# Two plain-form indices at the head of each feed-forward layer, and one index made ahead of each round of down products

## The chip, the cores and the metric

The kernel runs on one core of a Trainium2 chip. The metric is the device time of one execution in microseconds (us), lower is better; times are medians over runs of the kernel.

## What is computed

Two transformer-like blocks follow one another, each of two layers. The change touches the feed-forward part of the first block's two layers only:

```python
for l in range(DEPTH):                       # DEPTH = 2
    ...                                      # mixer: attention and a recurrent branch
    hn = rms_norm(h, norm_ffn_g[l])
    g, u = jnp.split(hn @ w_gu[l], [D_FF], axis=-1)      # D_FF = 2816, D_MODEL = 1024
    h = h + (jax.nn.silu(g) * u) @ w_down[l]
return h[:, N_META:, :]                      # then the second block
```

Everything is float32. Activations are held transposed: 1024 features as 8 tiles of 128 partitions, and 528 tokens (16 + 512) as columns. In the second layer only the last 512 tokens are needed, so that layer works on 512 columns.

## The kernel before

**Precision.** A float32 product is made of three matmuls: each operand is divided into a rounded part and a remainder (`hi`, `lo`), and `mm3` (L104) adds hi x hi, hi x lo, lo x hi. `split` (L188) makes the two: ScalarE copies `hi` (L189), VectorE subtracts (L190). Weights go the same way: `weight` (L95) loads 128 x 1024 values, copies on ScalarE (L99), subtracts on VectorE (L101). The tiles `wraw`, `whi`, `wlo` have 3 buffers each.

**One index.** The 2816 hidden features are 22 indices of 128. An index needs two weight tiles, gate and up. The plain way would be, for each of the two tiles and each half of the tokens (`n0`, `n1`, 264 or 256 columns), 8 feature tiles x 3 matmuls: 2 x 2 x 24 = 96 matmuls. The kernel uses seven products of quarters in place of eight (`seven`, L160): 7 x 4 x 3 = 84 matmuls. For that it needs sums of weight quarters, made on GpSimd in `halves4` (L133, four operations, L144 to L147), and sums of operand quarters, made once per layer (`ts`, divided into `th`, `tl`). The seven products land in PSUM (`av` one bank; `two`, 3 buffers of two banks), are added up on VectorE into `quarters` (L178 to L185), go through Silu on ScalarE (L691) and a product on GpSimd (L692), and are divided by `split` into `yh{i}`, `yl{i}`.

**The head of the layer.** After the norm (L229 to L244, with a chain of small VectorE operations, `rsqrt`, L203 to L216) VectorE scales each of 8 feature tiles into `g` (L655), first for `n0`, then for `n1`; `split` writes `xa` (`xh_all`, `xl_all`). The seven-product form needs, over `n1`, differences in place of some values: `g[k]` over `n1` is replaced for k < 4 (L668), and three sums for each k < 4 are made by GpSimd (L664, L672) and VectorE (L665).

**The down products.** The 22 indices run in chunks of 6, 6, 5, 5. After the last index of a chunk, for each of 8 output tiles m, a weight tile `w1dn` is loaded, both halves are multiplied with the chunk's `yh`, `yl` on TensorE, and VectorE adds the result to `h` (L704).

**Order.** The framework places waits and orders the instructions of each engine at compile time by a priority that follows the program text, with operations taken ahead of their place where its planner sees them ready. In the trace GpSimd's weight sums of the first two indices (L144 to L147) run beside the norm. Each engine then executes its own instructions in that fixed order, and every DMA of weights is issued by one queue (SP).

Of the kernel before, what the change touches and what calls it, by code (L numbers as in the profile page):

```python
# [9 lines left out]
F32 = mybir.dt.float32  # L10
F32R = mybir.dt.float32r
BF = mybir.dt.bfloat16
I32 = mybir.dt.int32
AF = mybir.ActivationFunctionType
# [6 lines left out]
T = S + NM  # L21
# [25 lines left out]
def both_blocks(ctx: ExitStack, tc: tile.TileContext, xT, cst, par1, w1in, w1out, w1gu, w1dn, wgate,  # L47
                memT, pos, par2, rel, w2in, w2mix, w2mq, w2mkv, w2mo, w2f1, w2f2, out):
    nc = tc.nc
# [4 lines left out]
    psum = None  # L54

    def open_psum(name):
        nonlocal psum, banks
        banks.close()
        banks = ExitStack()
        psum = banks.enter_context(tc.tile_pool(name=name, bufs=1, space=bass.MemoryType.PSUM))  # L60
# [2 lines left out]
    EARLY = 4  # L63
    BANKS = {"mm": 3, "sc": 2, "tr": 1, "av": 1, "bc": 1}
    EXTRA = {"mix1": None, "ff1": None, "mix2": "tr", "cross": "tr", "ff2": None}
    extra, turns = None, {}

    ALL = [(0, 264), (264, 528)]
    REAL = [(16, 528)]
# [22 lines left out]
    def f(ap):  # L92
        return ap.bitcast(F32)

    def weight(src, kt=8, eng=None):  # L95
        raw = wpool.tile([128, 8, 128], F32, name="wraw", bufs=3)
        nc.sync.dma_start(raw[:, :kt], src)
        hi = wpool.tile([128, 8, 128], F32R, name="whi", bufs=3)
        nc.scalar.copy(hi[:, :kt], raw[:, :kt])  # L99
        lo = wpool.tile([128, 8, 128], F32R, name="wlo", bufs=3)  # L100
        (eng or nc.vector).tensor_sub(lo[:, :kt], raw[:, :kt], f(hi[:, :kt]))  # L101
        return hi, lo

    def mm3(ps, wh, wl, xh, xl, first, last):  # L104
        nc.tensor.matmul(ps, wh, xh, start=first, stop=False)  # L105
        nc.tensor.matmul(ps, wh, xl, start=False, stop=False)  # L106
        nc.tensor.matmul(ps, wl, xh, start=False, stop=last)  # L107

    def bank(name):
        n = turns[name] = turns.get(name, 0) + 1  # L110
        if name == extra and n % (BANKS[name] + 1) == 0:
            name = "bc"
        return psum.tile([128, 512], F32, name=name, bufs=BANKS[name])
# [74 lines left out]
    def split(hi, lo, x):  # L188
        nc.scalar.copy(hi, x)  # L189
        nc.vector.tensor_sub(lo, x, f(hi))  # L190
# [68 lines left out]
    def tables():  # L259

        with tc.tile_pool(name="tab", bufs=1, side="right") as tb:
            halfpi = tb.tile([128, 1], F32)
            nc.vector.memset(halfpi, math.pi / 2)
            pi = tb.tile([128, S], I32)
            nc.sync.dma_start(pi, bass.AP(tensor=pos.tensor, offset=pos.offset, ap=[[0, 128], [1, S]]))
            pf = tb.tile([128, S], F32)
            nc.vector.tensor_copy(pf, pi)
            for n in range(2):
                ang = tb.tile([128, S], F32, name="ang")
                tn = tb.tile([128, S], F32, name="tn")  # L270
                if n:
                    co = sm.tile([128, S], F32, name="co")
                    si = sm.tile([128, S], F32, name="si")
                else:
                    co, si = cos1[:, :S], sin1[:, :S]
                nc.vector.tensor_scalar(ang, pf, inv[:, 2 * n:2 * n + 1], None, op0=OP.mult)
                nc.vector.tensor_scalar(tn, ang, 1 / (2 * math.pi), 12582912.0, op0=OP.mult, op1=OP.add)
                nc.vector.tensor_scalar(tn, tn, -12582912.0, None, op0=OP.add)
                for part in TWO_PI:
                    nc.vector.scalar_tensor_tensor(ang, tn, -part, ang, op0=OP.mult, op1=OP.add)  # L280
                nc.vector.tensor_scalar(ang, ang, math.pi - 1e-7, -(math.pi - 1e-7), op0=OP.min, op1=OP.max)
                nc.scalar.activation(si, ang, AF.Sin)
                nc.vector.tensor_scalar(si, si, inv[:, 2 * n + 1:2 * n + 2], None, op0=OP.mult)
                nc.scalar.activation(ang, ang, AF.Abs)
                nc.scalar.activation(co, ang, AF.Sin, bias=halfpi, scale=-1.0)
                tabs.append((co, si))
# [24 lines left out]
    for l in range(2):  # L311
# [4 lines left out]
        with ExitStack() as lay:  # L316
# [322 lines left out]
            with ExitStack() as ffn:  # L639
                share("ff1")  # L640
                open_psum("psum_f")
                ff = ffn.enter_context(tc.tile_pool(name="ff", bufs=1))
                r2 = small.tile([128, T], F32, name="rbc", bufs=1)
                for p, a, b in rnorm(small, sumsq(small, h, l0, T), l0, T, one2, D, 1e-6):
                    nc.scalar.copy(r2[:, a:b], p)
                half = (T - l0) // 2
                n0, n1 = slice(l0, l0 + half), slice(l0 + half, T)
                th, tl = (ff.tile([128, 4, 3, half], F32R, name=n) for n in ("th", "tl"))
                with tc.tile_pool(name="tq", bufs=1, side="right") as tq:
                    g = [None] * 8  # L650

                    def scaled(k, n):
                        if g[k] is None:
                            g[k] = tq.tile([128, T], F32, name=f"g{k}")
                        nc.vector.scalar_tensor_tensor(g[k][:, n], h[k][:, n], col(G_FFN + k), r2[:, n], op0=OP.mult, op1=OP.mult)  # L655

                    for k in range(8):
                        scaled(k, n0)
                        split(xa[k][0][:, n0], xa[k][1][:, n0], g[k][:, n0])
                    ts = [tq.tile([128, 3, half], F32, name=f"tt{k}") for k in range(4)]  # L660
                    for k in range(4):
                        scaled(k + 4, n1)
                        scaled(k, n1)
                        nc.gpsimd.tensor_sub(ts[k][:, 0], g[k][:, n1], g[k][:, n0])  # L664
                        nc.vector.tensor_sub(ts[k][:, 1], g[k + 4][:, n1], ts[k][:, 0])  # L665
                        split(th[:, k, :2], tl[:, k, :2], ts[k][:, :2])
                    for k in range(4):
                        nc.gpsimd.tensor_sub(g[k][:, n1], g[k + 4][:, n1], g[k][:, n1])  # L668
                        split(xa[k][0][:, n1], xa[k][1][:, n1], g[k][:, n1])
                    for k in range(4):  # L670
                        split(xa[k + 4][0][:, n1], xa[k + 4][1][:, n1], g[k + 4][:, n1])
                        nc.gpsimd.tensor_sub(ts[k][:, 2], g[k + 4][:, n0], ts[k][:, 1])  # L672
                        split(th[:, k, 2], tl[:, k, 2], ts[k][:, 2])
                quarters = [[[x[k][:, n] for k in ks] for x in zip(*xa)]
                            for ks, n in ((range(4), n0), (range(4, 8), n0), (range(4, 8), n1), (range(4), n1))]
                turned = [[[t[:, k, j] for k in range(4)] for t in (th, tl)] for j in range(3)]
                rhs = quarters[0], quarters[1], turned[1], turned[0], quarters[3], quarters[2], turned[2]
                if l == 1:
                    sm = blk2.enter_context(tc.tile_pool(name="sm", bufs=1, side="right"))
                fy = ffn.enter_context(tc.tile_pool(name="fy", bufs=1, side="right"))  # L680
                f0 = 0
                for nf in (6, 6, 5, 5):
                    if l == 1 and f0 == 6:
                        tables()
                    ys = []
                    for i in range(nf):
                        w = halves4(ff, w1gu[l, 2 * (f0 + i)], w1gu[l, 2 * (f0 + i) + 1])
                        e = seven(ff, w, rhs, half, 2 if l else 3)
                        sg, su = (e[:, o:o + 2].rearrange("p a b -> p (a b)") for o in (0, 2))
                        sl = ff.tile([128, T], F32, name="sl", bufs=1)  # L690
                        nc.scalar.activation(sl[:, l0:], sg, AF.Silu)  # L691
                        nc.gpsimd.tensor_mul(su, su, sl[:, l0:])  # L692
                        hi = fy.tile([128, T], F32R, name=f"yh{i}")
                        lo = fy.tile([128, T], F32R, name=f"yl{i}")
                        split(hi[:, l0:], lo[:, l0:], su)
                        ys.append((hi, lo))
                    for m in range(8):
                        w = weight(w1dn[l, m, :, f0:f0 + nf], nf)
                        ps = pair_of_banks()[:, :, :half]
                        for j, n in enumerate((n0, n1)):  # L700
                            for k, (yh, yl) in enumerate(ys):
                                mm3(ps[:, j], w[0][:, k], w[1][:, k], yh[:, n], yl[:, n], k == 0, k == nf - 1)
                        t = h[m][:, l0:].rearrange("p (a b) -> p a b", a=2)
                        nc.vector.tensor_add(t, t, ps)  # L704
                    f0 += nf
# [617 lines left out]
```

## Time and profile before

| | us |
|---|---|
| median of 3 runs | 2926.09 |
| lowest, highest | 2921.92, 2927.14 |
| the profiled execution's own time | 2924.17 |
| its span, first to last instruction | 2922.4 |
| mean granted TensorE clock (1 is 2.4 GHz) | 0.978 |
| feed-forward part of layer 0, from the norm's first matmul | about 279 to 680 |
| feed-forward part of layer 1 | about 927 to 1330 |

The profile is of one execution. An engine's "busy" is time in which it executes. A matmul's own duration overlaps that of its neighbours, so counts of matmuls per stretch are the better measure of TensorE's progress. PE is TensorE, DVE VectorE, ACT ScalarE, POOL GpSimd. "PEclk" is the clock that was granted, as a share of 2.4 GHz; 0.5 is 1.2 GHz.

### The profile page before, as it was taken

What the parts mean: (1) busy time and instruction counts of PE and PEld (TensorE: products, weight loads), DVE (VectorE), ACT (ScalarE), POOL (GpSimd) and SP (SyncE); (2) the same over time, 40 slices, a digit from 0 to 9 for tenths busy, and PEclk for the clock granted to TensorE, in tenths of its full rate; (3) what the DMA queues carried; (4) which work ended last, traced back from release to release, by engine and by line L of the source; (5) the groups of instructions that cost most, each with busy time, mean ns of one, the idle gap of its engine ahead of it and who ended that gap; (6) DMA issues with size and microseconds to landing.
All of it is one profiled execution on the core that took longest, in us unless ns stands there. A gap on an engine that the chain in (4) does not pass through costs nothing.

```text
span 2922.4 us, 46047 instructions
## 1 busy us (share of the span) xinstructions
PE 2763.0 (95%) x17604; PEld 2465.2 (84%) x17604; DVE 1939.8 (66%) x3702; ACT 1319.7 (45%) x2354; POOL 752.5 (26%) x647
## 2 busy tenths in 40 slices
PE   8988799999997899999999999999989999999998
PEld 7887799999875899998788888888877898888887
DVE  7887856667888855666988564333589875643335
ACT  6664433346664433343675434322346754433323
POOL 0012635450112644542202021111322120311112
PEclk9998899999998899999999999999999999999999
DMA  4332132223332233324613322333245242233222
GB/s 146 84 82 73 55 101 91 90 85 101 103 85 72 73 100 93 91 82 126 170 59 124 107 67 92 94 94 98 89 120 152 66 131 87 65 95 100 94 94 65
DMA packets 98813, 277.39 MB, mean 95 GB/s; under 512 B 13601, under 2 KB 20257, under 8 KB 98593
## 3 DMA queue, kind: packets, MB, share of 16 engines
q1 hardware_dynamic: 98592, 274.45, 31.2%
q8 instruction: 139, 2.28, 0.3%
q14 instruction: 82, 0.66, 0.1%
HBM read 241.82 MB, written 2.10 MB: 83 GB/s over the span
## 4 chain that ended last, share of the span: by engine, by line
PE 73%; DVE 13%; issue 5%; POOL 4%; ACT 3%; DMA 1%; SPq 0%; ACTq 0%; DVEq 0%; POOLq 0%
PE mm L106 16%; PE mm L107 16%; PE mm L105 16%; PE two L107 4%; PE two L105 4%; PE two L106 4%; POOL quarters L692 2%; PE av L105 1%; PE av L106 1%; PE av L107 1%; PE av L229 1%; POOL ws L147 1%; DVE wlo L101 1%; DVE wlo L190 1%; PE bc L927 1%
## 5 line engine op out<-in xcount | busy, mean ns | idle before, releaser
L99 ACT CAST whi<-wraw 128x1024 fp32r<-128x1024 f32 (+3 forms) x388 | 375.0, 970 | 635.9 <-PE mm L106 496.4
L105 PE MATMUL mm<-xh_all,whi 128*128 128x512 f32 (+2 forms) x1696 | 588.3, 349 | 14.6 <-ACT xh_all L328 7.1
L106 PE MATMUL mm<-xl_all,whi 128*128 128x512 f32 (+2 forms) x1696 | 591.2, 350 | 1.3 <-DVE xl_all L845 0.8
L107 PE MATMUL mm<-xh_all,wlo 128*128 128x512 f32 (+2 forms) x1696 | 588.4, 348 | 0.0
L101 DVE TENSOR_TENSOR wlo<-wraw,whi 128x1024 fp32r<-128x1024 f32 (+3 forms) x365 | 442.0, 1211 | 205.5 <-ACT whi L99 203.1
L105 PEld LDWEIGHTS mm<-xh_all,whi 128*128 128x128 f32 x1696 | 321.2, 190 | 53.1 <-ACT xh_all L328 7.1
L106 PEld LDWEIGHTS mm<-xl_all,whi 128*128 128x128 f32 x1696 | 322.1, 190 | 38.4 <-DVE xl_all L845 1.6
L107 PEld LDWEIGHTS mm<-xh_all,wlo 128*128 128x128 f32 x1696 | 323.0, 191 | 34.6
L1206 POOL TENSOR_TENSOR r<-r 128x512 f32<-128x512 f32 (+1 forms) x70 | 101.8, 1455 | 532.3 <-ACT r L1205 532.3
L105 PE MATMUL two<-yh,whi 128*128 128x264 f32 (+1 forms) x704 | 203.1, 290 | 17.8 <-ACT yh L189 16.3
L107 PE MATMUL two<-yh,wlo 128*128 128x264 f32 (+1 forms) x704 | 201.8, 288 | 0.0
L106 PE MATMUL two<-yl,whi 128*128 128x264 f32 (+1 forms) x704 | 201.3, 287 | 0.0
L106 PE MATMUL two<-tl,whi 128*128 128x264 f32 (+1 forms) x528 | 152.6, 289 | 4.3 <-DVE tl L190 4.3
L105 PE MATMUL two<-th,whi 128*128 128x264 f32 (+1 forms) x528 | 151.5, 288 | 5.0 <-ACT th L189 4.9
L107 PE MATMUL two<-th,wlo 128*128 128x264 f32 (+1 forms) x528 | 152.1, 288 | 4.1 <-DVE wlo L190 4.1
L105 PEld LDWEIGHTS two<-yh,whi 128*128 128x128 f32 x704 | 136.0, 194 | 20.4 <-ACT yh L189 18.0
L190 DVE TENSOR_TENSOR wlo<-wraw,whi 128x1024 fp32r<-128x1024 f32 x88 | 135.4, 1538 | 18.8 <-ACT whi L189 18.8
L773 DVE TENSOR_TENSOR hall<-hall,mm 128x512 f32<-128x512 f32 (+1 forms) x82 | 46.6, 568 | 146.0 <-PE mm L107 146.0
L106 PEld LDWEIGHTS two<-yl,whi 128*128 128x128 f32 x704 | 135.8, 193 | 0.1
L107 PEld LDWEIGHTS two<-yh,wlo 128*128 128x128 f32 x704 | 135.8, 193 | 0.0
L144 POOL TENSOR_TENSOR ws<-wraw 128x512 f32<-128x512 f32 x44 | 64.9, 1476 | 201.9 <-DMA wraw<-w1gu 129.0
L189 ACT CAST whi<-wraw 128x1024 fp32r<-128x1024 f32 x88 | 92.3, 1049 | 54.1 <-PE two L106 51.2
(718 smaller groups left out, 7574.5 us busy)
## 6 DMA issues: line engine op xcount, KB each, us to landing
wraw<-w2f SPq DMA_DIRECT2D x128, 512.0 KB, 3.9
wraw<-w1gu SPq DMA_DIRECT2D x88, 512.0 KB, 3.5
wraw<-w2in SPq DMA_DIRECT2D x44, 512.0 KB, 3.7
wraw<-w1in SPq DMA_DIRECT2D x40, 512.0 KB, 3.5
wraw<-w2mkv SPq DMA_DIRECT2D x32, 512.0 KB, 3.5
wraw<-w1dn SPq DMA_DIRECT2D x32, 384.0 KB, 3.1
wraw<-w1dn SPq DMA_DIRECT2D x32, 320.0 KB, 2.9
wraw<-w1out SPq DMA_DIRECT2D x32, 256.0 KB, 2.8
```

What stands on the lines that cost most here:

```text
L99: nc.scalar.copy(hi[:, :kt], raw[:, :kt])
L101: (eng or nc.vector).tensor_sub(lo[:, :kt], raw[:, :kt], f(hi[:, :kt]))
L105: nc.tensor.matmul(ps, wh, xh, start=first, stop=False)
L106: nc.tensor.matmul(ps, wh, xl, start=False, stop=False)
L107: nc.tensor.matmul(ps, wl, xh, start=False, stop=last)
L144: nc.gpsimd.tensor_add(s[:, 4:], r2[:, :4], r2[:, 4:])
L147: nc.gpsimd.tensor_sub(s4, r1[:, 4:], s[:, :4])
L189: nc.scalar.copy(hi, x)
L190: nc.vector.tensor_sub(lo, x, f(hi))
L692: nc.gpsimd.tensor_mul(su, su, sl[:, l0:])
L773: nc.vector.tensor_add(X(m, a, b), X(m, a, b), p)
L1206: nc.gpsimd.tensor_mul(r[:, a:b], r[:, a:b], r[:, a:b])
```

## The change

- The operands of both halves are scaled and divided first, in plain form, on VectorE and ScalarE. All sums of operand quarters (16 operations, four for each k < 4) then go to GpSimd; before, four of the 16 were VectorE's.
- `early()` makes the layer's indices 0 and 1 in plain form, 8 groups of 24 matmuls from four weight tiles; its PSUM tiles are halves of `two`. Silu is read from PSUM, and the product with Silu is VectorE's.
- The divisions of the sums (`th`, `tl`) and the rewritten `xa` over `n1` for k < 4 stand behind `early()`.
- The three engines' work on index 2's weights is kept behind the last division of the plain operands (`issue_after`; on GpSimd behind a copy of one column, `spot`).
- Chunks are 5, 5, 4, 4, 4, and before a chunk's down products the next chunk's first index is made.

```diff
     def open_psum(name):
-        nonlocal psum, banks
+        nonlocal psum, banks, paired, halves
+        paired, halves = name == "psum_f", None
...
+    halves = None
+
     def bank(name):
+        nonlocal halves
+        if name == "mm" and paired:
+            if halves is None:
+                got = psum.tile([128, 2, 512], F32, name="two", bufs=3)
+                halves = got[:, 1]
+                return got[:, 0]
+            got, halves = halves, None
+            return got
...
+                spot = ff.tile([128, 1], F32, name="spot")
+                firsts = [ff.tile([128, 4, half], F32, name="quarters", bufs=2 if l else 3) for _ in range(2)]
+
+                def early():
+
+                    ws = [weight(w1gu[l, t]) for t in range(3)]
+                    for t, n, j in ((0, n0, 0), (1, n0, 0), (2, n0, 0), (0, n1, 1), (1, n1, 1), (2, n1, 1), (3, n0, 0), (3, n1, 1)):
+                        if t == 3 and j == 0:
+                            ws.append(weight(w1gu[l, 3]))
+                        e = firsts[t // 2]
+                        for p, a, b in proj(ws[t], xa, [(n.start, n.stop)]):
+                            if t % 2:
+                                nc.vector.tensor_mul(e[:, 2 + j], e[:, j], p)
+                            else:
+                                nc.scalar.activation(e[:, j], p, AF.Silu)
+
...
-                    for k in range(8):
-                        scaled(k, n0)
-                        split(xa[k][0][:, n0], xa[k][1][:, n0], g[k][:, n0])
+                    for n in (n0, n1):
+                        for k in range(8):
+                            scaled(k, n)
+                            hi, lo = xa[k]
+                            after = [nc.scalar.copy(hi[:, n], g[k][:, n]),
+                                     nc.vector.tensor_sub(lo[:, n], g[k][:, n], f(hi[:, n]))]
+                    after.append(nc.gpsimd.tensor_copy(spot, g[7][:, T - 1:T]))
                     ts = [tq.tile([128, 3, half], F32, name=f"tt{k}") for k in range(4)]
                     for k in range(4):
-                        scaled(k + 4, n1)
-                        scaled(k, n1)
                         nc.gpsimd.tensor_sub(ts[k][:, 0], g[k][:, n1], g[k][:, n0])
-                        nc.vector.tensor_sub(ts[k][:, 1], g[k + 4][:, n1], ts[k][:, 0])
-                        split(th[:, k, :2], tl[:, k, :2], ts[k][:, :2])
+                        nc.gpsimd.tensor_sub(ts[k][:, 1], g[k + 4][:, n1], ts[k][:, 0])
+                        nc.gpsimd.tensor_sub(g[k][:, n1], g[k + 4][:, n1], g[k][:, n1])
+                        nc.gpsimd.tensor_sub(ts[k][:, 2], g[k + 4][:, n0], ts[k][:, 1])
+                    early()
                     for k in range(4):
-                        nc.gpsimd.tensor_sub(g[k][:, n1], g[k + 4][:, n1], g[k][:, n1])
+                        split(th[:, k], tl[:, k], ts[k])
                         split(xa[k][0][:, n1], xa[k][1][:, n1], g[k][:, n1])
-                    for k in range(4):
-                        split(xa[k + 4][0][:, n1], xa[k + 4][1][:, n1], g[k + 4][:, n1])
-                        nc.gpsimd.tensor_sub(ts[k][:, 2], g[k + 4][:, n0], ts[k][:, 1])
-                        split(th[:, k, 2], tl[:, k, 2], ts[k][:, 2])
...
-                f0 = 0
-                for nf in (6, 6, 5, 5):
-                    if l == 1 and f0 == 6:
-                        tables()
-                    ys = []
-                    for i in range(nf):
-                        w = halves4(ff, w1gu[l, 2 * (f0 + i)], w1gu[l, 2 * (f0 + i) + 1])
+                made = []
+
+                def index(i):
+                    if i < 2:
+                        su = firsts[i][:, 2:4].rearrange("p a b -> p (a b)")
+                    else:
+                        with ExitStack() as order:
+                            if i == 2:
+                                for ins in after:
+                                    order.enter_context(tc.issue_after(ins.ins))
+                            w = halves4(ff, w1gu[l, 2 * i], w1gu[l, 2 * i + 1])
...
+                    hi = fy.tile([128, T], F32R, name=f"yh{i % 6}")
+                    lo = fy.tile([128, T], F32R, name=f"yl{i % 6}")
+                    split(hi[:, l0:], lo[:, l0:], su)
+                    made.append((hi, lo))
+
+                f0 = 0
+                for nf in (5, 5, 4, 4, 4):
+                    if l == 1 and f0 == 5:
+                        tables()
+                    while len(made) < min(f0 + nf + 1, 22):
+                        index(len(made))
+                    ys = made[f0:f0 + nf]
```

## Rows read from the trace of the kernel before

**Rows 1.** The page: the span, and each engine's busy time, share and instructions
```profile
span 2922.4 us, 46047 instructions
PE 2763.0 (95%) x17604; PEld 2465.2 (84%) x17604; DVE 1939.8 (66%) x3702; ACT 1319.7 (45%) x2354; POOL 752.5 (26%) x647
```
**Rows 2.** TensorE's waits, layer 0, 288 to 680: total us, times, longest
```profile
PE two L105 <- ACT yh L189: 8.1, 4, 2.4
PE two L106 <- DVE xl_all L190: 7.5, 1, 7.5
```
**Rows 3.** TensorE's waits, layer 1, 926 to 1340
```profile
PE two L105 <- ACT yh L189: 8.2, 4, 2.3
```
**Rows 4.** Stretches of layer 0: PE, PEld, DVE, ACT, POOL busy (instructions), PEclk, DMA, GB/s
```profile
290.00:297.00 7.00, 5.33 (x23) 5.01 (x24) 6.73 (x19) 5.22 (x12) 0.00 (x0) 0.52 0.02 4
290.00:330.00 40.00, 23.68 (x134) 22.06 (x135) 37.41 (x72) 19.25 (x39) 19.93 (x18) 0.66 0.12 36
...
370.00:390.00 20.00, 17.61 (x132) 17.39 (x131) 11.64 (x16) 5.79 (x10) 5.44 (x4) 0.91 0.35 104
400.00:420.00 20.00, 20.00 (x167) 20.00 (x166) 9.96 (x11) 5.34 (x6) 9.29 (x6) 1.00 0.32 102
480.00:500.00 20.00, 17.55 (x130) 17.15 (x129) 9.62 (x13) 4.59 (x6) 2.58 (x2) 0.91 0.35 100
```
**Rows 5.** Stretches of layer 1, same columns
```profile
938.00:945.00 7.00, 5.60 (x22) 5.14 (x23) 6.74 (x19) 5.14 (x13) 0.05 (x1) 0.50 0.00 0
938.00:974.00 36.00, 25.69 (x136) 23.07 (x137) 33.75 (x57) 18.13 (x36) 20.48 (x17) 0.66 0.14 41
...
1024.00:1034.00 10.00, 7.31 (x48) 6.93 (x48) 5.40 (x7) 2.09 (x3) 2.55 (x2) 0.83 0.41 120
1044.00:1064.00 20.00, 20.00 (x171) 20.00 (x170) 9.25 (x10) 4.37 (x6) 9.21 (x6) 1.00 0.33 107
1124.00:1144.00 20.00, 17.31 (x131) 16.86 (x130) 9.90 (x13) 4.79 (x7) 2.55 (x2) 0.91 0.34 100
1204.00:1244.00 40.00, 36.51 (x289) 35.72 (x289) 23.19 (x30) 12.95 (x19) 11.99 (x10) 0.96 0.31 90
```
**Rows 6.** Timeline beside layer 0's norm: start, us, engine, line, operation, operands [idle before]
```profile
282.43 1.28 POOL L145 TENSOR_TENSOR ws<-ws,wraw 128x512 f32<-128x512 f32 x1
...
282.62 1.12 DVE L209 TENSOR_SCALAR nwt<-nwt 88x12 f32<-88x12 f32 x1
283.77 1.18 DVE L211 SCALAR_TENSOR_TENSOR nwu<-nwt 88x12 f32<-88x12 f32 x1
...
284.99 2.40 DVE L214 SCALAR_TENSOR_TENSOR nwu<-nwu,nwt 88x12 f32<-88x12 f32 x2
```
**Rows 7.** All instructions of L211: count, ns min/median/max, first and last start
```profile
L211 DVE SCALAR_TENSOR_TENSOR nwu<-nwt x42: 135/159/1189, 24.6 to 2913.3; 88x12 f32<-88x12 f32 x20, 128x4 f32<-128x4 f32 x12, 128x8 f32<-128x8 f32 x10
```
**Rows 8.** Timeline at layer 0's head: operands scaled and divided, then sums
```profile
293.50 1.29 DVE L655 SCALAR_TENSOR_TENSOR g<-hall,par,rbc 128x264 f32<-128x264 f32 x3
...
295.81 0.78 DVE L190 TENSOR_TENSOR xl_all<-g,xh_all 128x264 fp32r<-128x264 f32 x2 [0.27 <-ACT xh_all L189]
...
297.07 0.93 POOL L664 TENSOR_TENSOR tt<-g 128x264 f32<-128x264 f32 x1 [7.11 <-DVE g L655]
...
298.21 0.97 DVE L665 TENSOR_TENSOR tt<-g,tt 128x264 f32<-128x264 f32 x1
```
**Rows 9.** Timeline, ScalarE's copies: sums, rewritten operand, weight
```profile
299.55 0.63 ACT L189 CAST th<-tt 128x528 fp32r<-128x528 f32 x1
...
301.54 0.41 ACT L189 CAST xh_all<-g 128x264 fp32r<-128x264 f32 x1
...
319.51 1.04 ACT L189 CAST whi<-ws 128x1024 fp32r<-128x1024 f32 x1 [8.99 <-PE two L106]
```
**Rows 10.** Timeline, TensorE in layer 0: a late weight, and the first chunk's end
```profile
358.29 0.39 PE L107 MATMUL av<-xh_all,wlo 128*128 128x264 f32 x1 [1.40 <-DVE wlo L190]
...
384.54 0.39 PE L105 MATMUL two<-yh,whi 128*128 128x264 f32 x1 [2.38 <-ACT yh L189]
```

More of the change, by code (lines that the diff above doesn't have):

```diff
@@ L65, in both_blocks @@
     EXTRA = {"mix1": None, "ff1": None, "mix2": "tr", "cross": "tr", "ff2": None}
-    extra, turns = None, {}
+    extra, turns, paired = None, {}, False
     ALL = [(0, 264), (264, 528)]
@@ L692, in both_blocks @@
                         nc.gpsimd.tensor_mul(su, su, sl[:, l0:])
[L693 to L696, printed above, removed]
+                    hi = fy.tile([128, T], F32R, name=f"yh{i % 6}")
[9 more added lines that the diff above has]
+                    ys = made[f0:f0 + nf]
                     for m in range(8):
```

## The prediction

> **What bounds the kernel now.** I read the page first, then TensorE's waits over each feed-forward part, then the stretches, and only then single instructions. TensorE is busy for 95% of the span, more than any other engine [rows 1], so time can only come from stretches where it is not at its rate. That rate is read in the middle of a chunk: 167 matmuls in 20 us in layer 0, 0.120 us each, and 171 in layer 1, 0.117 us each, clock 1.00 [rows 4, 5]. Against it two places stand out. First, the head of each layer: of 40 us from 290 to 330 TensorE gets 134 matmuls done, 16 us worth, at a mean clock of 0.66; in layer 1 136 in 36 us, again at 0.66 [rows 4, 5]. The longest wait there is for a divided operand, 7.5 us in one piece [rows 2]. Second, the end of each chunk: four waits in each layer, 8.1 and 8.2 us in all, for `yh`, the last index of the chunk on its way through Silu, product and division [rows 2, 3]; the first of them, 2.38 us, is in [rows 10]. The clock falls after these: 0.91, 0.91, 0.83, 0.96 in the stretches around them [rows 4, 5].
>
> **The norm ahead of the head.** The change keeps GpSimd's weight sums out of the norm. Beside such a sum a VectorE operation on 88 x 12 values took 1.18 us, and two of L214 2.40 us together [rows 6]; the median over the kernel of the same kind is 0.159 us [rows 7]. Three of these are 3.1 us too long; two more of the chain are as slow by the same pattern, some 5 us in all. Against that VectorE now has two more weight tiles to subtract at this point. I take 4 us earlier in each layer (bounds 0 and 5).
>
> **The plain head, layer 0.** I compare where index 2 can begin, which is after 168 matmuls before and after 192 now.
> - Before: 134 at 330, the other 34 at 0.120 us: 334.1.
> - Now: the first group of 24 is fed by the operands over `n0`, the same instructions as before, the last of them done at 296.6 [rows 8], when TensorE had done 23 by 297 [rows 4]. With 4 us off: 293. Two more groups over `n0` are 48 x 0.120 = 5.8 us, to 298.8, at full clock because TensorE doesn't stop.
> - The operands over `n1` are 16 VectorE operations from 292.6 on. Alone such an operation takes 0.43 (scaling, three in 1.29) or 0.39 us; with a GpSimd sum beside it 0.97 us [rows 8]. The ends are 16 x 0.41 = 6.6 us and 16 x 0.97 = 15.5 us; GpSimd's sums can start once the first `n1` tile is there, so part of this runs beside them, and I take the middle, 11 us: 303.6. The group that streams behind them ends at 304.0.
> - Four groups are left: 96 x 0.120 = 11.5 us, so the plain form ends at 315.5 (312.5 to 324).
> - GpSimd's 16 sums at 0.93 us [rows 8] are 15 us, from about 295 to 310, under this work. The divisions of the sums follow, 0.63 us for 528 columns, so about 0.85 us for 792. But the four rewritten `xa` over `n1` can be written only when the last group has read them, and in ScalarE's queue they stand between the divisions of the sums, ahead of `yh0`, `yh1` and index 2's weights. If everything waits there, behind the last group's start come 3 x 0.85 + 4 x 0.41 + 2 x 0.63 + 1.04 us [rows 9], 6.5 us, and VectorE's subtractions as many: up to 7 us of restart beyond the end of the group. If the planner takes the sums ahead, it is 0, because index 2's first two products use only operands that aren't rewritten. I take 4 us.
> - Index 2 then begins at 319.5: 14.6 us earlier than before (bounds 3 and 22).
>
> **The plain head, layer 1.** Before: 136 at 974, 32 more at 0.117: 977.7. Now: operands over `n0` done at about 945 less 4 us [rows 5], 16 operations of 0.69 us on the mean (11 us) to 952, 0.4 us, 96 x 0.117 = 11.2 us, 4 us of restart: 967.6. Gain 10 us (bounds -1 and 18).
>
> **The later indices of the first chunk.** TensorE already waits for a late weight in this chunk, 1.40 us in [rows 10]. Before, two indices' weights were prepared ahead; now index 2's begin only behind the plain operands and GpSimd's 16 sums, and four indices in a row have to be fed from there. No row shows this order. The nearest is that wait; I take two more such waits in each layer, -6 us together (0 to -12).
>
> **The chunk ends.** With one index made ahead, the chunk's last `yh` has 10 us (84 x 0.120) in which to be finished, where 2.38 us were lacking. Three of the four waits of a layer go; the fourth, at the layer's end, has nothing to put ahead of it and stays. That is 3 x 2.2 us per layer, 13 us in all. The clock comes with it: 1 less 0.91 over 20 us is 1.8 us, twice in layer 0; 1.7, 1.8 and 1.6 us in layer 1 [rows 4, 5]; 8.7 us. Of 22 us I take 20 (10 to 23), as some of the wait could move to the weights of the down products. The fifth chunk adds eight weight tiles and eight VectorE additions per layer; they lie beside the 24 matmuls (2.9 us) of each output tile, while VectorE is busy half of such a stretch [rows 4], and I price them at 0 (to -3). The number of down matmuls doesn't change, and the weight queue on SP carries the same bytes. The four operand sums that move from VectorE to GpSimd relieve the engine that is late at the head; their cost is in GpSimd's 15 us.
>
> **Sum.** 14.6 + 10 - 6 + 20 = 39 us. The profiled execution took 2924.17 us, so 2885; the median of the runs is 2 us higher, so **2887 us**.
>
> **The rivals.**
>
> *A. GpSimd and VectorE take turns over the whole `n1` phase.* For it: 0.97 against 0.39 to 0.43 us [rows 8], and the slow chain of the norm [rows 6, 7]. Against it: GpSimd needs tiles that VectorE hasn't made yet, and stands still for them. If each of the 16 operations waits for a sum, a pair costs 0.93 + 0.41 = 1.34 us and the phase 21.4 us: index 2 begins at 292.6 + 21.4 + 0.4 + 11.5 + 4 = 329.9 in layer 0, 4 us of gain, and at about 978 in layer 1, none. 4 - 6 + 20 = 18 us, 2908 us. The Trainium skill has a rule of this kind: by "SBUF — State Buffer", section "Who interferes with whom", a VectorE instruction with two SBUF inputs and a GpSimd instruction that reads SBUF exclude each other, and the one that comes second stands still until the first is done. That speaks against moving sums to GpSimd beside this phase, and would make this rival the forecast if GpSimd always had a sum ready. The trace agrees on the pairs that overlap, at 0.97 us, and goes further in one respect, as the norm's L209, with one input, took 1.12 us [rows 6].
>
> *B. The order doesn't come out as written.* The planner may leave the down products ahead of the index that is meant to cover the gap, or the wait may reappear for weights. Then the chunk ends give nothing: 2926 - (24.6 - 6) = 2907 us. For it: the planner takes work out of its place, as the weight sums beside the norm show [rows 6]. Against it: in the trace of before the wait sits exactly where the program puts it [rows 10].
>
> *C. Slower: GpSimd becomes the bound of the head.* It has the 16 sums, and index 2's four weight sums behind them, while VectorE is near full (37.4 of 40 us [rows 4]) and may hold it off. At a mean of 2.9 us per sum, three times the row's 0.93, the sums run from 295 to 341, index 2's weight sums and divisions to about 348, and index 2 begins 14 us later than before, in both layers: 28 - 20 = 8 us slower, 2934 us. It decides from a sum of 2.6 us on, where the later start takes the 20 us of the chunk ends. Nothing in the trace shows a sum of this size near that.
>
> **How the numbers follow.** A measurement of this kernel can tell about 0.2%, 6 us, from no change. Forecast 75%, its own range 2868 to 2904 (best heads and chunk ends on one side, 7 us of restart and slow operands on the other); A 13%, B 8%, C 4%. All but C end below 2920, yet several costs at their worst at once would take most of the gain: faster 0.90, same 0.06, slower 0.04. The range reaches to A and B: 2866 to 2910.
>
> **What the profile of the changed kernel would show.** The norm: L211 and L214 in both layers near 0.16 us, with no GpSimd sum beside them. The head: matmuls on `xh_all` without a hole of over 2 us, PEclk near 1.0 from the second group on, and the last plain group ending near 315 in layer 0 (layer 1 by its own start, 28 us later). The restart: TensorE idle for 0 to 7 us ahead of index 2, released by ScalarE or VectorE. The chunk ends: one wait for `yh` in each layer in place of four, and no stretch at 0.91 or below after the head. I would be wrong if a wait as long as the old ones stood at each new chunk end under another name, if index 2 began later than 330, or if the later indices of the first chunk waited over 3 us each for weights.

## The result

The change takes 2881.4 us (median of 4 runs, 2880.19 to 2885.76) against 2924.06 us for the kernel before in the same measurement: a ratio of 0.9856, with a 95% interval of 0.9839 to 0.9873, or 42.7 us less. The forecast was 2887 us, in a range of 2866 to 2910.

The total came out near the sum; the terms did not. The page of the changed kernel, its first lines:

```profile
span 2883.9 us, 46217 instructions
PE 2761.7 (96%) x17652; PEld 2467.3 (86%) x17652; DVE 1926.9 (67%) x3710; ACT 1323.9 (46%) x2366; POOL 719.8 (25%) x637
```

There are 48 matmuls more than before (24 per layer: 192 in plain form for 168) and TensorE is busy for 1 us less [rows 1]: what went is time in which it stood. Its waits in layer 0 (276 to 680) and in layer 1 (880 to 1320), as total us, times, longest:

```profile
PE two L106 <- DVE quarters L672: 8.0, 1, 8.0
...
PE bc L255 <- DVE nwy L227: 1.9, 1, 1.9
...
PE two L106 <- ACT yh L200: 0.9, 1, 0.9
...
PE two L106 <- DVE quarters L672: 3.8, 1, 3.8
```

Of four waits for `yh` in a layer, 8.1 and 8.2 us [rows 2, 3], one of 0.9 us is left in each. But a wait stands at the head that wasn't there before: 8.0 and 3.8 us for L672, the product with Silu of the plain form. The stretches show the rest (columns as in [rows 4]); the first three lie in the head of layer 0, the last at the first chunk's end:

```profile
297.00:305.00 8.00, 4.65 (x23) 3.14 (x23) 8.00 (x11) 2.97 (x4) 8.00 (x10) 0.85 0.02 4
305.00:310.00 5.00, 5.00 (x23) 4.83 (x23) 4.92 (x4) 2.94 (x5) 5.00 (x4) 0.56 0.00 0
310.00:318.00 8.00, 0.04 (x1) 0.00 (x0) 7.79 (x17) 3.68 (x5) 7.04 (x6) 0.68 0.00 0
...
375.00:395.00 20.00, 20.00 (x167) 20.00 (x166) 9.51 (x13) 5.43 (x8) 7.50 (x6) 1.00 0.32 98
```

The head gets 46 matmuls done in the 13 us from 297 to 310 and one in the 8 us after, at a granted clock that falls to 0.56 (0.5 is 1.2 GHz). The chunk end runs at 167 in 20 us, the full rate, where it was 132 at 0.91 [rows 4].

To see where the time went I cut both traces at the same events: the first matmul of a feed-forward layer's norm, the first matmul of index 2 on `th` (24 matmuls into index 2 in either form), and the last addition of the down products. Of the kernel before:

```profile
279.29 1.54 PE L229 MATMUL av<-one,ss_acc 128*88 128x2 f32 x12 [2.16 <-DVE ss_acc L254]
...
337.09 0.29 PE L105 MATMUL two<-th,whi 128*128 128x264 f32 x1
...
686.25 0.70 DVE L704 TENSOR_TENSOR hall<-hall,two 128x528 f32<-128x528 f32 x1 [0.17 <-PE two L107]
926.59 1.02 PE L229 MATMUL av<-one,ss_acc 128*128 128x2 f32 x8 [2.54 <-DVE ss_acc L254]
...
980.67 0.28 PE L105 MATMUL two<-th,whi 128*128 128x256 f32 x1
...
1329.56 0.69 DVE L704 TENSOR_TENSOR hall<-hall,two 128x512 f32<-128x512 f32 x1 [1.30 <-PE two L107]
```

And of the changed kernel:

```profile
279.23 1.89 PE L240 MATMUL av<-one,ss_acc 128*88 128x2 f32 x12 [2.99 <-DVE ss_acc L265]
...
332.39 0.29 PE L106 MATMUL two<-th,whi 128*128 128x264 f32 x1
...
664.45 0.70 DVE L743 TENSOR_TENSOR hall<-hall,two 128x528 f32<-128x528 f32 x1
909.56 1.26 PE L240 MATMUL av<-one,ss_acc 128*128 128x2 f32 x8 [2.99 <-DVE ss_acc L265]
...
962.52 0.28 PE L106 MATMUL two<-th,whi 128*128 128x256 f32 x1
...
1288.20 0.69 DVE L743 TENSOR_TENSOR hall<-hall,two 128x512 f32<-128x512 f32 x1 [0.49 <-PE two L108]
```

From the norm to index 2 it is 57.8 and 54.1 us before, 53.2 and 53.0 us now: the two heads together gave 5.8 us, not 24.6. A feed-forward layer as a whole went from 407.0 to 385.2 and from 403.0 to 378.6 us, 46.1 us together. And the mixer between them, which the change doesn't touch, went from 240.3 to 245.1 us. The same cuts for all kernels of this study, in us:

| kernel | median | ratio to before (95%) | layer 0 | mixer | layer 1 |
|---|---|---|---|---|---|
| before | 2924.06 | 1 | 407.0 | 240.3 | 403.0 |
| the change | 2881.4 | 0.9856 (0.9839 to 0.9873) | 385.2 | 245.1 | 378.6 |
| ends_only | 2896.93 | 0.9909 (0.9895 to 0.9924) | 393.9 | 244.2 | 386.8 |
| head_only | 2905.16 | 0.9934 (0.9917 to 0.9951) | 399.1 | 240.6 | 394.1 |
| none_ahead | 2906.4 | 0.9934 (0.9914 to 0.9955) | 391.6 | 243.7 | 390.7 |
| own_banks | 2877.16 | 0.9841 (0.9826 to 0.9855) | 381.7 | 244.9 | 374.1 |
| params_held | 2886.59 | 0.9872 (0.9857 to 0.9887) | 384.9 | 244.6 | 381.5 |
| sums_late | 2880.13 | 0.9849 (0.9831 to 0.9868) | 383.8 | 243.7 | 376.5 |
| no_hold | 2880.09 | 0.9849 (0.9829 to 0.9868) | 382.6 | 245.1 | 376.6 |
| last_five | 2876.2 | 0.9837 (0.9815 to 0.986) | 385.0 | 241.1 | 377.4 |
| own_five | 2870.07 | 0.9816 (0.9801 to 0.983) | 379.7 | 240.9 | 375.9 |
| own_five_free | 2870.38 | 0.9817 (0.9801 to 0.9833) | 380.6 | 241.1 | 373.0 |

Medians are compared through the ratio, since the kernel before was run again beside each group. Two kernels whose ratios differ by 0.0015, 4 us, can't be told apart by their intervals; the cuts, each from one profiled execution, say where such a difference lies.

### The profile page after: what moved, and what is told of

Same layout as the page of the kernel before. It is cut to its first block, busy times and chain, and to the rows that moved or that the text cites. A ratio compares the mean times of both kernels' runs of the same rounds, so it can differ in the third digit from the quotient of the medians.

```text
span 2883.9 us, 46217 instructions
## 1 busy us (share of the span) xinstructions
PE 2761.7 (96%) x17652; PEld 2467.3 (86%) x17652; DVE 1926.9 (67%) x3710; ACT 1323.9 (46%) x2366; POOL 719.8 (25%) x637
## 4 chain that ended last, share of the span: by engine, by line
PE 78%; DVE 12%; issue 3%; POOL 3%; ACT 2%; DMA 1%; ACTq 0%; DVEq 0%; POOLq 0%; SPq 0%
PE mm L107 16%; PE mm L108 16%; PE mm L106 16%; PE two L108 6%; PE two L106 6%; PE two L107 6%; PE av L106 1%; PE av L107 1%; PE av L108 1%; DVE wlo L102 1%; PE av L240 1%; DVE wlo L201 1%; DVE sq L481 1%; PE av L851 1%; PE bc L966 1%
## 5 line engine op out<-in xcount | busy, mean ns | idle before, releaser
L100 ACT CAST whi<-wraw 128x1024 fp32r<-128x1024 f32 (+2 forms) x412 | 386.2, 941 | 627.5 <-PE mm L107 504.8
L102 DVE TENSOR_TENSOR wlo<-wraw,whi 128x1024 fp32r<-128x1024 f32 (+2 forms) x389 | 458.2, 1179 | 209.5 <-ACT whi L100 208.4
L106 PEld LDWEIGHTS mm<-xh_all,whi 128*128 128x128 f32 x1696 | 323.7, 192 | 53.2 <-ACT xh_all L339 7.1
L106 PE MATMUL two<-xh_all,whi 128*128 128x264 f32 (+1 forms) x448 | 133.5, 301 | 18.4 <-DVE quarters L672 11.8
L107 PE MATMUL two<-xl_all,whi 128*128 128x264 f32 (+1 forms) x448 | 134.1, 300 | 4.1 <-DVE xl_all L689 4.1
L107 PE MATMUL two<-tl,whi 128*128 128x264 f32 (+1 forms) x480 | 136.2, 284 | 0.0
L108 PE MATMUL two<-th,wlo 128*128 128x264 f32 (+1 forms) x480 | 136.1, 283 | 0.0
L106 PE MATMUL two<-th,whi 128*128 128x264 f32 (+1 forms) x480 | 135.9, 283 | 0.0
L108 PE MATMUL two<-xh_all,wlo 128*128 128x264 f32 (+1 forms) x448 | 132.7, 297 | 2.2 <-DVE wlo L102 1.2
L201 DVE TENSOR_TENSOR wlo<-wraw,whi 128x1024 fp32r<-128x1024 f32 x80 | 119.7, 1496 | 21.2 <-ACT whi L200 20.8
```

## Experiments: the two parts alone

Two theories stood against each other: the prediction's (heads 25 less 6, chunk ends 20) and one from the changed kernel's trace (heads 5, chunk ends the rest).

**ends_only**: the head of before, the new chunk ends.

```diff
-                for nf in (6, 6, 5, 5):
+                for nf in (5, 5, 4, 4, 4):
...
+                    while len(made) < min(f0 + nf + 1, 22):
+                        index(len(made))
+                    ys = made[f0:f0 + nf]
```

> The head of before (all 22 indices in the seven-product form, sums as before) with the chunks of the change: 5, 5, 4, 4, 4 and one index made ahead of each round of down products. By the terms of the prediction the chunk ends are worth 20 us and the heads 25 less 6: about 2904 us. By a reading of the changed kernel's trace it is the other way round: from index 2 on its TensorE waits for 0.9 us in layer 0 and 2.8 us in layer 1, where the kernel before lost some 15 and 20 us, and its heads are only about 5 us shorter in all: then this kernel alone brings 30 to 38 us, 2886 to 2894 us.

2896.93 us, 26.5 us less than the 2923.47 beside it: between the two theories. The layers are 13.1 and 16.2 us shorter, and the mixer is 3.9 us longer.

**head_only**: the new head, the old chunks.

```diff
-                for nf in (5, 5, 4, 4, 4):
+                for nf in (6, 6, 5, 5):
...
-                    while len(made) < min(f0 + nf + 1, 22):
+                    while len(made) < f0 + nf:
```

> The head of the change with the chunks of before (6, 6, 5, 5, no index ahead). By the terms of the prediction 19 us faster than before, 2905 us. If the plain head gains little, because TensorE stands for 8.0 us in layer 0 and 3.8 us in layer 1 in the middle of it, it is 3 to 10 us faster, 2914 to 2921 us, with four waits for yh in each layer as before.

2905.16 us, 18.3 us less: the prediction's figure to the microsecond, though the head itself is short of it. Index 2 begins 53.3 us after the norm in layer 0 and 51.7 us in layer 1, 4.5 and 2.4 us earlier than before. The first wait for `yh` shows what came on top:

```profile
277.75 1.45 PE L240 MATMUL av<-one,ss_acc 128*88 128x2 f32 x9 [2.99 <-DVE ss_acc L265]
...
331.01 0.29 PE L106 MATMUL two<-th,whi 128*128 128x264 f32 x1
...
374.48 0.39 PE L106 MATMUL two<-yh,whi 128*128 128x264 f32 x1 [2.40 <-ACT yh L200]
```

From the norm to that matmul it is 96.7 us, against 384.54 - 279.29 = 105.3 us before [rows 10]: 8.5 us gained by then, so 4 us of them in indices 2 to 5. Layer 1 has the same, 95.5 against 104.2 us. The waits for late weights in the first chunk, such as the 1.40 us of [rows 10], are gone in layer 0. The two parts add up: 26.5 + 18.3 = 44.8 against 42.7 us.

**none_ahead**: the change without the index made ahead.

```diff
-                    while len(made) < min(f0 + nf + 1, 22):
+                    while len(made) < f0 + nf:
```

> The changed kernel (plain head, chunks 5, 5, 4, 4, 4) without the index made ahead. If the order at the chunk ends is what the chunk part of the change brings, four waits of 2.0 to 2.4 us for yh per layer come back beside the last, with their clock loss, and the time is 20 to 26 us above the change, 2901 to 2908 us, as with the chunks of before (2905). If the fifth chunk has a price of its own, it is above 2908 us. The mixer between the two layers took 4 to 5 us longer in both kernels with the new chunk ends than in both with the old: if the five chunks do that, it is 244 us here too, if the index ahead does it, 240 us.

2906.4 us, 25 us above the change. Each layer has five waits for `yh`, shorter than forecast (0.9 to 2.0 us) but 6.7 us together in layer 0:

```profile
PE two L106 <- ACT yh L200: 6.7, 5, 1.7
```

So it is the index ahead that pays at the chunk ends; the chunks' new lengths bring nothing. The mixer took 243.7 us here too: the chunks, not the index ahead, lengthen it.

**last_five**: the change with the layer's last chunk as long as it was.

```diff
-                for nf in (5, 5, 4, 4, 4):
+                for nf in (5, 4, 4, 4, 5):
```

> The changed kernel with chunks 5, 4, 4, 4, 5 in place of 5, 5, 4, 4, 4, so that the layer ends with five k per output tile as before. If the mixer's extra 4 to 5 us come from the shorter last chunk (less time per output tile for the next layer's first operands), the mixer takes 240 to 241 us and the kernel 3 to 5 us less than the change, 2876 to 2879 us. If not, the time is that of the change, 2880 to 2884 us.

2876.2 us, mixer 241.1 us. The same 1493 matmuls of the mixer, from the last addition to the next norm's first matmul; first this kernel, then the change:

```profile
662.30:903.30 241.00, 228.78 (x1493) 197.19 (x1493) 205.61 (x498) 146.41 (x273) 31.49 (x47) 1.00 0.34 95
```

```profile
664.50:909.60 245.10, 230.09 (x1493) 198.67 (x1493) 208.10 (x500) 148.05 (x275) 29.05 (x47) 0.99 0.33 94
```

The total alone doesn't show it, since the interval of this kernel overlaps that of the change; the mixer does: it takes 240.3 to 241.1 us in the five kernels of the table whose last chunk has five indices (k), and 243.7 to 245.1 us in the seven whose last chunk has four. GpSimd's 47 instructions of the mixer are the same ones in both kernels, at other times relative to the layer's end. By what chain the shorter chunk does this I didn't follow.

## Experiments: the wait in the plain head

**own_banks**: a PSUM tile for each of the eight plain groups, in place of the halves of a pair.

```diff
         if name == "mm" and paired:
-            if halves is None:
-                got = psum.tile([128, 2, 512], F32, name="two", bufs=3)
-                halves = got[:, 1]
-                return got[:, 0]
-            got, halves = halves, None
-            return got
+            halves = (halves or 0) + 1
+            if halves in (4, 5):
+                return psum.tile([128, 512], F32, name="av" if halves == 4 else "bc", bufs=1)
+            return psum.tile([128, 2, 512], F32, name="two", bufs=3)[:, 0]
```

> The changed kernel, but each of the eight plain groups takes a PSUM tile of its own (three of two, av, bc, three of two) in place of halves of a pair. If TensorE's 8.0 us and 3.8 us come from this, that the second half of a pair is written only when the first half has been read by the late product on VectorE, both go to under 1.5 us, the clock stays at full, and the kernel takes 8 to 15 us less than the change, 2866 to 2873 us. If something else holds the groups at that place (the operands over n1, the fourth weight tile), a wait of like length stands under another name and the time stays at 2878 to 2884 us.

The mechanism is confirmed: the waits for L672 are gone in both layers, and index 2's first matmul on `th` comes 46.0 and 43.0 us after the norm, 11.8 and 11.1 us earlier than before the change. In layer 0, a late weight and that matmul:

```profile
321.46 0.39 PE L108 MATMUL av<-xh_all,wlo 128*128 128x264 f32 x1 [1.90 <-DVE wlo L199]
...
325.35 0.42 PE L106 MATMUL two<-th,whi 128*128 128x264 f32 x1
```

The forecast of the time was missed: 2877.16 us is 4 us below the change, less than the intervals can tell apart. Written as halves of one tile, the second group of a pair starts only after the first has been read, and the reading product stood late in VectorE's queue. The changed kernel's VectorE shows where (with next to it ScalarE, on whose Silu the product rests):

```profile
311.06 1.12 DVE L383 TENSOR_SCALAR gs<-par 128x8 f32<-128x8 f32 x1
...
312.18 1.23 DVE L399 TENSOR_SCALAR lc<-par 128x4 f32<-128x4 f32 x1
...
314.65 1.19 DVE L393 TENSOR_TENSOR lc<-lc 128x4 f32<-128x4 f32 x1
315.88 1.18 DVE L396 TENSOR_TENSOR lc<-lc 128x4 f32<-128x4 f32 x1
...
317.58 0.43 DVE L672 TENSOR_TENSOR quarters<-quarters,two 128x264 f32<-128x264 f32 x1
```

```profile
308.00 1.28 ACT L388 ACT_TABLE_LOAD   x1
309.29 0.20 ACT L388 ACTIVATE lc<-lc 128x4 f32<-128x4 f32 x1
309.51 1.28 ACT L674 ACT_TABLE_LOAD   x1
310.81 0.39 ACT L674 ACTIVATE quarters<-two 128x264 f32<-128x264 f32 x1
```

These are parameters of the next layer, taken ahead by the planner: 7.9 us of small operations in front of a product that TensorE waits for, slowed by the GpSimd sums beside them, and an exponential of four columns that costs ScalarE two table loads. Of the 17 us by which the two heads became earlier than the change's, 9 us are lost again before the first matmul on `yh`: from index 2's first matmul on `th` to it are 40.7 and 44.2 us, in the change 38.0 and 37.8. TensorE now stands for weights of index 2 and of later ones (1.90 us for `wlo` in layer 0; 1.31, 1.85 and 1.91 us in layer 1). In the change no wait for weights behind index 2's start is over 0.5 us in the first chunk: in layer 0, GpSimd made index 2's weight sums from 307 to 317 us, while TensorE stood.

**params_held**: the pairs stay, the next layer's small operations and the tables are kept behind the plain head (`last` holds the head's last product and last Silu).

```diff
+            with ExitStack() as hold:
+                for ins in last:
+                    hold.enter_context(tc.issue_after(ins.ins))
...
-                        tables()
+                        with tc.issue_after(last[0].ins), tc.issue_after(last[1].ins):
+                            tables()
```

> The changed kernel with the next layer's small VectorE and ScalarE operations (L370 to L402) and the tables kept behind the last product and the last Silu of the plain head; the pairs stay. If TensorE's 8.0 us are the time for which the product stood in VectorE's queue behind those small operations (309.7 to 317.5), the wait falls to under 2 us and the kernel gains 6 to 10 us, 2871 to 2876 us. If ScalarE's Silu of the group before is what is late, the wait falls by less than half and the time by less than 4 us.

A miss: 2886.59 us, no faster than the change. The wait in layer 0 became 4.3 us and a second one of 1.8 us for the fourth weight tile:

```profile
PE two L106 <- DVE quarters L676: 4.3, 1, 4.3
...
PE two L108 <- DVE wlo L102: 1.8, 1, 1.8
```

With the small operations away, a division of a weight sum of index 2 stood in front of the product. It waited 4.27 us for ScalarE's copy, and that for GpSimd's sum:

```profile
314.79 1.09 DVE L201 TENSOR_TENSOR wl<-ws,wh 128x512 fp32r<-128x512 f32 x1 [4.27 <-ACT wh L200]
```

So it is the pair that makes the product urgent: without the small operations something else stood in its way, and without the pair (own_banks) the wait was gone.

**sums_late**: on top of own_banks, all operand sums behind VectorE's work on `n1`.

```diff
-                    for k in range(4):
-                        nc.gpsimd.tensor_sub(ts[k][:, 0], g[k][:, n1], g[k][:, n0])
...
+                    with tc.issue_after(after[2].ins):
+                        for k in range(4):
+                            nc.gpsimd.tensor_sub(ts[k][:, 0], g[k][:, n1], g[k][:, n0])
...
```

> The kernel with a PSUM tile of its own for each plain group, and all 16 operand sums kept behind the one-column copy, that is behind VectorE's work on the operands over n1. If GpSimd and VectorE shut each other out there (VectorE took 13.8 us for 16 operations and their like with the sums beside them), VectorE is done with n1 in 7 to 8 us, TensorE's waits for xl_all and xh_all from 297 to 303 vanish. If that carries through, the kernel takes 4 to 10 us less than its parent, 2867 to 2873 us; if the sums, now some 6 us later, hold up index 2's operands and weights by as much, the time stays at 2875 to 2880 us.

VectorE's scaling of six tiles, first in the changed kernel with GpSimd's sums beside it, then here without:

```profile
291.15 5.01 DVE L682 SCALAR_TENSOR_TENSOR g<-hall,par,rbc 128x264 f32<-128x264 f32 x6
...
296.09 5.48 DVE L689 TENSOR_TENSOR xl_all<-g,xh_all 128x264 fp32r<-128x264 f32 x6
```

```profile
291.55 2.52 DVE L680 SCALAR_TENSOR_TENSOR g<-hall,par,rbc 128x264 f32<-128x264 f32 x6
294.00 2.15 DVE L687 TENSOR_TENSOR xl_all<-g,xh_all 128x264 fp32r<-128x264 f32 x6
```

0.84 and 0.91 us each against 0.42 and 0.36: half the speed. The work on `n1` ends some 7 us earlier and TensorE's waits for it vanish. Yet the time is 2880.13 us, no better than its parent. In layer 0, index 2's first product waits 1.6 and 1.9 us for its weights, and its second 5.5 us for a Silu (L672 of that kernel):

```profile
323.77 0.59 PE L106 MATMUL two<-xh_all,whi 128*128 128x264 f32 x1 [5.55 <-ACT quarters L672]
```

In ScalarE's queue that Silu stood behind the copy of a weight sum, for which ScalarE had waited 6.1 us for GpSimd, and behind the two table loads. The gain went into the next wait, by the second way that the expectation names: the later operand sums put the weight sums some 4 us later.

**no_hold**: the change without the hold on index 2's weights.

```diff
-                            if i == 2:
+                            if i == 2 and False:
                                 for ins in after:
```

> The changed kernel without the hold on index 2's weights; seven weight sums then stand ahead of the operand sums in GpSimd's order. If these sums beside the norm are what made its VectorE chain slow, the chain is back at 6 to 7 us in place of 1.8 in layer 0, and the kernel is 4 to 9 us slower than the change, 2885 to 2891 us. If the early weights give the time back in the first chunk, it is within 3 us of the change.

Both halves of the expectation came true together. The norm's chain is slow again (TensorE waits 7.3 and 9.7 us for its end in place of 1.9 and 2.6), and still the kernel takes 2880.09 us, that of the change: with the weight sums made early, the waits for L672 in layer 0 are 0.7 and 0.3 us and index 2 has its weights. In layer 0:

```profile
289.56 0.70 PE L255 MATMUL bc<-cs,nwy 88*128 88x88 f32 x3 [7.27 <-DVE nwy L227]
...
318.65 0.39 PE L106 MATMUL two<-xh_all,whi 128*128 128x264 f32 x1 [0.74 <-DVE quarters L672]
```

What the hold saves in the norm it costs in the head.

**own_five** and **own_five_free**: a tile for each group (own_banks's edit, not repeated here) and chunks 5, 4, 4, 4, 5, with and without the hold; the second pair of lines below is in own_five_free alone.

```diff
-                for nf in (5, 5, 4, 4, 4):
+                for nf in (5, 4, 4, 4, 5):
...
-                            if i == 2:
+                            if i == 2 and False:
```

> A PSUM tile of its own for each plain group together with chunks 5, 4, 4, 4, 5. The first gained 4 us on the change and the second 5 us; they act at different places (the head, the mixer after layer 0). If they add, 2871 to 2874 us; if the earlier head is paid back in waits for weights, no better than the second alone, 2875 to 2878 us.

> The same without the hold on index 2's weights, so that seven weight sums are made beside the norm and the norm's chain is slow again (about 5 us more per layer). If, with the pairs gone, late weights are what limits the head (TensorE's waits for whi and wlo at indices 2 to 4), these waits shrink to under 1 us in all and the kernel is 0 to 4 us faster than with the hold, in spite of the norm. If not, it is 5 to 9 us slower.

2870.07 us, the two gains add: 11 us below the change, with intervals that don't touch, and 1.8% below the kernel before. Its median is also below those of own_banks and last_five, but there the intervals overlap. Without the hold it is 2870.38 us, the same, where the expectation had 0 to 4 us faster or 5 to 9 us slower: TensorE waits 5 to 6 us longer for each norm, and in return its waits for index 2's weights are gone (3.9 and 3.2 us with the hold; later indices still wait 1.2 and 2.1 us).

## Why the prediction came out, step by step

- **What bounds the kernel**: right. The time came from the two places named, and full rate at the chunk ends is 167 per 20 us as read in [rows 4].
- **The norm, 4 us per layer**: right as a step. L222, the former L211, took 0.17 us in layer 0's norm, and the first scaling begins at 284.15 where it began at 288.80. As a price on the whole it was worth nothing: no_hold gives it up and loses no time, as its weight sums are done early and the wait of 8.0 us in layer 0's head shrinks to 1.0.
- **The operands over `n1`, 11 us (6.6 to 15.5)**: 15.2 us, from 289.72 to 304.94, near the upper bound, in which 1.9 us went to a division and a product of later work. The sums overlapped more than assumed, but the start was 2.9 us earlier than forecast, so the end came 1.3 us later. Rival A names the right mechanism: sums_late shows twice the speed with GpSimd away. The trace agrees with the rule of the Trainium skill, "SBUF — State Buffer", section "Who interferes with whom", on these instructions with two SBUF inputs. The prediction takes the norm's L209, with one input, to go beyond it; the same section of the Trainium skill lists `tensor_scalar` among the operations that can contend, so it need not. As a cause that decides the time the rival fell: taking the overlap away gained nothing, at least where it is done by making the sums later; no other way was run.
- **Four groups at full rate behind them, 11.5 us**: this step failed. It assumed that TensorE doesn't stop. It stood for 8.02 us because of the halves of `two`, as own_banks shows, and ran at a granted clock of 0.50 for 5 us behind that. (The slow stretch ahead of it, 0.56, follows the wait for operands over `n1`: own_banks has 0.56 from 303 to 310 too.) The last plain group ended near 330, where 315.5 was forecast. I had the pairing in the diff and priced it at nothing. Without it the heads come out near the forecast: own_banks has 11.8 and 11.1 us of gain, for 14.6 and 10.
- **Restart, 4 us (0 to 7)**: 0. In layer 0 the planner put index 2's first matmuls ahead of the last plain group, and from 318 to index 2's first on `th` TensorE waits for nothing. The sums of its weights were made while TensorE stood; their subtractions (319.7 to 325.7) and the rewriting of `xa` (327.9 to 329.8) lay beside the last two plain groups.
- **Index 2 earlier by 14.6 and 10 us**: 4.6 and 1.1 us, within the bounds given (3 to 22, -1 to 18) but far below the values taken.
- **Later indices of the first chunk, -6 us**: the sign was wrong. In head_only they gave 4.0 and 6.3 us: the waits for late weights that stood there before went, because the pause gave the weights their time. That it is the pause shows in own_banks, which has no such pause: from index 2's first matmul on `th` to the first on `yh` the change gains 4.1 and 6.5 us on the kernel before, own_banks 1.5 and 0.2. This offsets most of the error of the head: 18.6 us were forecast for both terms, head_only brought 18.3.
- **Chunk ends, 20 us (10 to 23)**: 26.5 us in ends_only, above the upper bound: 29.3 us in the two layers, less 3.9 us in the mixer. The mechanism was right (three of four waits go, the fourth stays at 0.9 us, the clock holds at 1.00). The size was low in part because late weights at the start of a chunk's last index went too, as with 1.28 us at 471 in the kernel before, and because the fourth wait shrank, from 1.28 to 0.91 us in layer 0; what made up the rest was not traced.
- **The fifth chunk, 0 to -3 us**: 0 within the layer; in the mixer behind it 4 to 5 us were lost, which last_five gives back. That a chunk's length reaches into the next stage was not in the prediction.
- **Sum**: 39 us forecast, 42.7 measured. The direction and the size rest on two part totals that were near (18.6 for 18.3, 20 for 26.5); the split within the head was wrong in both of its terms, and that they cancelled was luck. The chunk ends' surplus was also offset in part by the mixer's loss of 4 to 5 us, which was not in the sum. Rivals B and C didn't occur: the waits at the chunk ends went, and GpSimd's sums were done by 307.

## What to carry to other kernels

Making the next unit of work ahead of a stage that waits for the last one's post-processing is cheap and paid in full here: 25 us for one line of order, where the same chunks without it gave nothing. A head that is filled with other matmuls is worth only as much as the next late thing allows: the waits taken away here (pair, sums, norm) handed most of their time to what was late behind them, weights above all, so price the chain of the next operand before the hole. Two groups in one PSUM tile are one tile to whoever places the waits: give a group its own tile when its reader is late in a queue.

## What the runs showed of the hardware beyond that

A VectorE operation on a few columns can be hit by GpSimd as a long one is: 0.14 to 0.17 us alone, 1.1 to 1.2 us beside a sum of 128 x 512, about the sum's own 1.25 us. Six of the fifteen in front of the late product were hit, and the fifteen took 7.9 us ahead of a product of 0.43 us. An exponential between two Silus cost ScalarE 2 x 1.28 us of table loads for 0.20 us of work. And a pause of 8 us cost TensorE more than its length: the granted clock was 0.95 just before it (309.4 to 309.9 us) and 0.50 in the 5 us behind it (318 to 323), in which 22 matmuls were done, where full rate is 42.
